# Sums of the opening's modulations formed as columns by TensorE, late operands pinned in the mixers, and later modulations in the merge

## The chip, the cores and the metric

The kernel runs on one core of a Trainium2 chip. The metric is the device time of one execution in microseconds (us), as the median of several runs; smaller is better. One further execution is taken with the hardware profiler, and its trace is what the views below read. The engines are TensorE (PE, the matrix engine; PEld is its weight load), VectorE (DVE), ScalarE (ACT), GpSimd (POOL) and SyncE (SP), whose queue issues most of the DMAs.

## The reference

One layer over 1024 latent tokens and 256 context tokens of width 1024: a half-step gated FFN, token mixers (a short gated convolution and grouped-query attention) merged by gates and an output projection, and a second half-step FFN. Each sub-layer is normalised and modulated: nine vectors of 1024 (shift, scale and gate, three times) come from SiLU(c) for the latents and from SiLU(c_ctx) for the context, by one product with `w_mod`.

```python
mod_lat = (jax.nn.silu(c) @ w_mod[layer] + b_mod[layer])[:, None, :]
mod_ctx = (jax.nn.silu(c_ctx) @ w_mod[layer] + b_mod[layer])[None, None, :]
ml = jnp.split(mod_lat, N_MOD, axis=-1)
mc = jnp.split(mod_ctx, N_MOD, axis=-1)
x = x + 0.5 * ml[2] * swiglu(modulate(rms_norm(x, norm1_g[layer]), ml[0], ml[1]),
                              ffn1_w_in[layer], ffn1_w_out[layer])
cx = cx + 0.5 * mc[2] * swiglu(modulate(rms_norm(cx, norm1_g[layer]), mc[0], mc[1]),
                                ffn1_w_in[layer], ffn1_w_out[layer])
hx = modulate(rms_norm(x, norm2_g[layer]), ml[3], ml[4])
hc = modulate(rms_norm(cx, norm2_g[layer]), mc[3], mc[4])
...
x = x + ml[5] * merge_branches(y_conv_l, o_l, gt_l, w_branch_conv[layer],
                               w_branch_attn[layer], w_out[layer])
x = x + 0.5 * ml[8] * swiglu(modulate(rms_norm(x, norm3_g[layer]), ml[6], ml[7]),
                              ffn2_w_in[layer], ffn2_w_out[layer])
return rms_norm(x, final_g)
```

With `modulate(h, shift, scale) = h * (1 + scale) + shift` and `swiglu(h, w_in, w_out) = (silu(a) * b) @ w_out`, a and b being the halves of `h @ w_in`. The context's merge and second FFN are not needed, as the layer is the last.

## The kernel before, in words

**Products.** Activations lie with the width over the 128 partitions, tokens along the row, in two chunks of 512 tokens, C0 and C1. A float32 operand is split into a high part rounded to the matmul's format (made by ACT, names ending in h, or the first of a pair) and a low part, the rest (made by DVE); a product is three matmuls, high by high, high by low and low by high. The large products (FFN1, the mixers' `w_in`, FFN2) are formed by the Winograd scheme of class `Winograd`: of the 2x2 blocks of weights and activations seven products are made, numbered 1 to 7, from sums and differences of blocks. Weights come as `raw` by DMA, `s` are sums of their blocks (POOL), `wl` the split weights; `r` are the split operands of the activations, `nt`, `t` and `h` the sums and blocks they are split from. `start` runs products 1 and 2 of the first `n_ahead` column pairs; `second` goes on with products 6, 7, 4 and the rest. While `start` runs, a generator (`norm`) makes the normalised operands of the later products, one step at each `run(norm, 1)`; its last steps make the operands of products 7, 4 and 3.

**Modulations.** They are made in three ways. In the opening, `column_mod` makes one half (512 columns) of modulations 1 and 0 for both streams by matmuls with `silu_c` (two columns, one per stream) as the loaded operand and `w_mod` (`rawm`) as the moving one; the result, two rows of 512, is copied by ACT (`mrow`) and transposed into columns, and `column_adds` adds the bias. `second_mod` makes the other half for the latents: DVE adds `rawm` times a scalar into `macc`, eight times, `acch` and `accl` are its split, two matmuls with a column of ones sum it over the partitions, and the row goes into columns as above. `later_mod` does likewise for all others, as a generator: eight steps that load a `rawm` and add it, four empty ones, the split, six empty ones, the sum, whose row goes into columns by small DMAs (`mcol`). Generators are pulled by `run(steps, n)`: `all_later_mods` in the loop of FFN1 over j, `STEPS[j]` steps a time and three in each pass of a side loop for the context, `late_steps` in the mixers' loop over i and in FFN2.

**Row products.** `row_products` multiplies the second matrix of an FFN: for each of the products 2, 1, 4, 6, 5, 7 and 3 over all its rows (`hid` from DRAM, split into `rh` and `rl`, weights `wl` and `wh`), and then adds the four results to their outputs (`add`, for instance x<-ps,gate_l,x). The context's own product is put among these as po<-hidc,wo, added into `cacc`.

**What sets the order.** The code issues instructions in order of its loops, and a scheduler moves them within each engine's stream. `pinned=True`, or `strict[0] = True` around a piece of code, keeps an instruction in the program's order. Buffers: `ttile` takes from one pool of 11 (macc, acch, accl, rawm, s, u, v and others share it); PSUM has five banks for ps, two for pt and one for po. All instructions go through one helper, so the line of nearly every row is 88, and rows are told apart by names.

Of the kernel before, what the change touches and what calls it, by code (L numbers as in the profile page):

```python
# [40 lines left out]
SIDE_FROM = 12  # L41
STEPS = (0, 4, 4, 4, 5, 5, 5, 5, 5, 5, 5, 2, 12)
WAIT = 4
# [6 lines left out]
def tile_dit_layer(  # L50
# [211 lines left out]
    def later_mod(m, halves=(0, 1), streams=None):  # L262
# [3 lines left out]
        for half in halves:  # L266
# [12 lines left out]
            for _ in range(WAIT):  # L279
                yield  # L280
            parts = []
            for acc in accs:
                ah, al = ttile("acch", dt=F32R), ttile("accl", dt=F32R)
                split(acc, ah, al)
                parts.append((ah, al))
            for _ in range(6):
                yield
            for (ah, al), v in zip(parts, streams):
                mod, pm = (modl, modc)[v], ps_t()
# [8 lines left out]
                dve.tensor_add(out=mod[:, c0 : c0 + 4], in0=mcol[:], in1=bcol[:, c0 : c0 + 4])  # L298
            yield

    def fetch_mod(m, half):
# [17 lines left out]
    def column_mod(m, half, raws, bank):  # L319

        sc = silu_c[:].rearrange("p (v k) -> p k v", k=KD)
        pr = bank()
        for k in range(KD):
            matmul(pr[:2], sc[:, k], raws[k // 2][:, k % 2], start=(k == 0), stop=(k == KD - 1))
            if k % 2 and k < KD - 1:
                yield
        row = ttile("mrow")
        act.copy(out=row[:2], in_=pr[:2])
        yield
        pm = ps_t(8)  # L330
        for j in range(4):
            transpose(pm[:, 2 * j : 2 * j + 2], row[:2, j * P : (j + 1) * P])
        column_adds(m, half, pm, (0, 1))
        yield

    def second_mod(m, half, raws):

        acc = ttile("macc")
        for k in range(KD):
# [15 lines left out]
        pm = ps_t(4)  # L355
        for j in range(4):
            transpose(pm[:, j : j + 1], row[:1, j * P : (j + 1) * P])
        column_adds(m, half, pm, (0,))
        yield
# [106 lines left out]
    class Winograd:  # L466
# [194 lines left out]
        def start(self, norm):  # L661

            for i in range(self.n_ahead):
                t = wpool.tile([P, 2, 512], F32, tag="wh", name=uniq("uc"), bufs=W_BUFS)
                u, c = t[:, 0], t[:, 1]
                act.copy(out=u, in_=self.product(1))
                run(norm, 2 if i == 0 else 1)
                dve.tensor_add(out=c, in0=u, in1=self.product(2))
                if i < RESIDENT:
                    self.started.append((u, c))  # L670
                else:
                    self.put_aside(t)
            run(norm, 9 - self.n_ahead)
            self.prefetch(4)
            self.late = norm
# [79 lines left out]
        def third(self, u, v):  # L755
# [39 lines left out]
    def row_products(w, rows, add, after=lambda i, k: None, halves=False):  # L795
# [112 lines left out]
        }  # L908
        chain = None
        for i in (2, 1, 4, 6, 5, 7) + (() if halves else (3,)):  # L910
# [3 lines left out]
            for g, (k, m) in enumerate(groups):  # L914
# [4 lines left out]
                strict[0] = True  # L919
                sums(i, g)  # L920
                strict[0] = False
                after(i, k)
            for o, ch in to[i]:
                for d in range(4):
                    add(o + d, ch, ps[d])
            after(i, rows.n)
        if halves:
            kept = []
            ps = [ps_s(256) for _ in range(4)]
            for k, m in groups:  # L930
                for lr in operands(3, k, m):
                    step(3, ps, len(kept), *lr, n=256)
                    kept.append(lr)
                after(8, k)
            for d in range(4):
# [110 lines left out]
    run(mod00)  # L1046
    part_gain(gain1["c"], 0, "g1", "c", 0, 4)
    mod11 = second_mod(1, 1, raws11)
    for k in range(4):
        left_operand(0, k, mod11)  # L1050
    start = half1.start_together()
    half1.prefetch(5, lo_engines=(pool, pool))
# [88 lines left out]
    def all_later_mods():  # L1141
# [153 lines left out]
    def after1(i, k):  # L1295
# [16 lines left out]
        if k == NH // 2:  # L1312
# [4 lines left out]
            elif i == 3:  # L1317
                done(range(4), C1)
        if i == 3 and k in (0, 4):
            run(norms2, 1)  # L1320
# [23 lines left out]
    for i in range(KD):  # L1344
# [581 lines left out]
```

## Time and profile before

| | us |
|---|---|
| median of 3 runs (2686.28 to 2688.88) | 2687.64 |
| the profiled run's own time | 2688.7 |
| its span in the trace | 2686.9 |
| PE busy | 2643.4 |
| DVE busy | 2007.1 |
| ACT busy | 1166.1 |
| POOL busy | 521.3 |
| mean granted clock of PE | 0.993 |

The stages follow one another on PE: opening (to about 60 us), FFN1 with the side loop (to 665), its row products (to about 935), the mixers, attention, the merge and the output projection (to about 2030), FFN2 and its row products (to the end). The granted clock is the share of full speed that PE was allowed in a stretch. In the timeline a row is a run of alike instructions with start and length; in brackets stands the idle time of the engine before it, and what ended it. A matmul's start-to-start distance can be less than its shown length, as they are pipelined.

### The profile page before, as it was taken

Reading aid. Unit: us, or ns where it says so; the run is one execution under the profiler, and the core shown is the slowest. Engines: PE = TensorE matmul, PEld = TensorE weight load, DVE = VectorE, ACT = ScalarE, POOL = GpSimd, SP = SyncE. Lnnn points to the kernel's source line nnn. Section 1 sums busy time; section 2 is a strip of 40 time slices with the busy share of each in tenths; the row PEclk is TensorE's granted clock in tenths of the full one; section 3 lists DMA queues with packets and bytes.
Section 4 is the critical chain, followed back from the end, with each engine's and each line's share of the span. In section 5 each row is a group of like instructions: output and inputs, shape, how many; then the busy total and the mean of one; then the engine's idle time right before and its main releaser. Section 6 shows DMA issues by size and latency. Waiting matters only on the chain.

```text
span 2686.9 us, 37399 instructions
## 1 busy us (share of the span) xinstructions
PE 2643.4 (98%) x13593; PEld 2236.0 (83%) x13593; DVE 2007.1 (75%) x3356; ACT 1166.1 (43%) x2317; POOL 521.3 (19%) x409
## 2 busy tenths in 40 slices
PE   8999999999999999999999999999999999999998
PEld 5788898888788877888999888877888888888888
DVE  5888888786887889877488666775458875667875
ACT  6633543333454632333244666674236333334543
POOL 1244012121110044232033111000001533230200
PEclk9999999999999999999999999999999999999998
DMA  7655653346973445433213211002524543228731
GB/s 267 236 180 166 223 184 124 109 130 240 293 169 102 149 137 165 134 114 116 97 48 103 95 62 49 24 25 78 167 85 146 184 145 99 83 90 305 165 83 63
DMA packets 369920, 364.84 MB, mean 136 GB/s; under 512 B 27830, under 2 KB 261448, under 8 KB 369736
## 3 DMA queue, kind: packets, MB, share of 16 engines
q1 hardware_dynamic: 360712, 345.17, 39.0%
q0 software_dynamic: 9024, 17.30, 4.0%
q8 instruction: 106, 1.74, 0.3%
q14 instruction: 78, 0.64, 0.1%
HBM read 296.30 MB, written 66.06 MB: 135 GB/s over the span
## 4 chain that ended last, share of the span: by engine, by line
PE 88%; DVE 6%; DMA 2%; ACT 2%; issue 1%; SPq 1%; POOL 0%; DVEq 0%; ACTq 0%; POOLq 0%
PE ps L88 73%; PE po L88 7%; PE pt L88 7%; DMA rawm<-in_w_mod_dram 1%; DVE macc L88 1%; DVE wl L88 1%; SPq L88 1%; DVE xb L88 0%; DVE r L88 0%; ACT r L88 0%; DMA raw<-in_ffn_w_in_dram 0%; DMA xtok<-in_ctx_dram 0%; DVE ol L88 0%; DVE x L88 0%; DVE pts L88 0%
## 5 line engine op out<-in xcount | busy, mean ns | idle before, releaser
L88 PE MATMUL ps<-r,wl 128*128 128x512 f32 x5232 | 1213.4, 392 | 11.6 <-ACT wl L88 6.8
L88 PEld LDWEIGHTS ps<-r,wl 128*128 128x128 f32 x5232 | 983.9, 189 | 220.0 <-ACT wl L88 9.0
L88 ACT CAST wl<-s 128x512 fp32r<-128x512 f32 x256 | 158.0, 620 | 338.3 <-PE ps L88 266.6
L88 POOL TENSOR_TENSOR s<-raw 128x512 f32<-128x512 f32 x64 | 92.4, 1444 | 993.8 <-PE ps L88 346.6
L88 ACT CAST wl<-raw 128x512 fp32r<-128x512 f32 x286 | 176.4, 619 | 250.0 <-PE ps L88 160.6
L88 DVE TENSOR_TENSOR wl<-raw,wl 128x512 fp32r<-128x512 f32 x284 | 202.6, 717 | 68.3 <-ACT wl L88 64.7
L88 DVE TENSOR_TENSOR wl<-s,wl 128x512 fp32r<-128x512 f32 x256 | 231.8, 906 | 12.3 <-ACT wl L88 10.7
L88 POOL TENSOR_TENSOR s<-raw,s 128x512 f32<-128x512 f32 x64 | 99.8, 1560 | 363.9 <-DVE wl L88 354.4
L88 DVE SCALAR_TENSOR_TENSOR macc<-rawm,silu_c,macc 128x512 f32<-128x512 f32 x168 | 137.9, 837 | 9.5 <-DMA rawm<-in_w_mod_dram 9.1
L88 PE MATMUL ps<-wh,r 128*128 128x256 f32 x768 | 141.6, 285 | 0.0
L88 DVE TENSOR_TENSOR pts<-pt,pts 128x512 fp32r<-128x512 f32 x160 | 108.8, 687 | 39.4 <-ACT pts L88 38.4
L88 DVE TENSOR_TENSOR u<-u,ps 128x512 f32<-128x512 f32 x168 | 114.2, 680 | 28.5 <-PE ps L88 28.4
L88 DVE TENSOR_REDUCE m<-ps 128x1 f32<-128x512 f32 (+1 forms) x192 | 110.9, 596 | 31.0 <-PE ps L88 30.3
L88 ACT CAST pts<-pt 128x512 fp32r<-128x512 f32 x160 | 93.2, 593 | 88.7 <-PE pt L88 86.8
L88 ACT CAST rh<-hid 128x512 fp32r<-128x512 f32 x132 | 81.6, 621 | 112.2 <-PE ps L88 96.2
L88 PE MATMUL ps<-rh,wl 128*128 128x512 f32 x360 | 122.0, 389 | 0.0
L88 PEld LDWEIGHTS ps<-wh,r 128*128 128x128 f32 x768 | 120.6, 192 | 0.0
L88 ACT CAST wh<-raw 128x512 fp32r<-128x512 f32 (+1 forms) x88 | 69.3, 795 | 103.0 <-PE ps L88 79.5
L88 PE MATMUL po<-pts,vh 128*128 128x512 f32 x256 | 110.5, 437 | 1.5 <-ACT pts L88 1.5
L88 DVE TENSOR_TENSOR rl<-hid,rh 128x512 fp32r<-128x512 f32 x132 | 90.1, 686 | 26.5 <-ACT rh L88 13.5
L88 PE MATMUL ps<-wl,r 128*128 128x256 f32 x384 | 108.8, 283 | 0.0
L88 PE MATMUL ps<-kl,qs 128*128 128x512 f32 x384 | 105.3, 397 | 0.0
(298 smaller groups left out, 5068.1 us busy)
## 6 DMA issues: line engine op xcount, KB each, us to landing
raw<-in_ffn_w_in_dram SPq DMA_DIRECT2D x125, 512.0 KB
raw<-in_ffn_w_out_dram SPq DMA_DIRECT2D x72, 512.0 KB
rawm<-in_w_mod_dram SPq DMA_DIRECT2D x128, 256.0 KB
raw<-in_w_in_dram SPq DMA_DIRECT2D x61, 512.0 KB
hid<-hd SPq DMA_DIRECT2D x40, 512.0 KB
ws<-in_ffn_w_out_dram POOLq DMA_DIRECT2D x30, 512.0 KB, 6.6
ucd<-uc SPq DMA_DIRECT2D x22, 512.0 KB
hd<-c SPq DMA_DIRECT2D x38, 256.0 KB
```

Of the source, the lines that this page charges most:

```text
L88: inst = getattr(self.engine, name)(*args, **kw)
```

## The change

The change has five parts.

1. In the opening, `column_mod` swaps the operands: blocks of `rawm` are loaded and the two columns of `silu_c` move, so the sum arrives as columns; the row's copy and its transposes are gone. `second_mod` sums `macc` the same way, against a column of ones, through the new `summed_mod`; its split, row and transposes are gone. `part_gain` for the context comes after the first left operand.
2. `later_mod` splits and sums one stream after the other, three empty steps behind each split.
3. `STEPS` is lower; m=5 moves from `all_later_mods` to `late_steps`, which is pulled less in the mixers (from i=3, two and two) and also in the merge, five steps behind each of 14 pieces.
4. `start` of the mixers takes no step of `norm` at i = 5, 6 and 8, and none at its end; `late_operands` runs the rest, pinned, inside the first `second`.
5. `row_products` adds a product's results behind the first sums of the next product, pinned (`add_results`), and the steps `norms2` come at k = 2 and 6.

```diff
-STEPS = (0, 4, 4, 4, 5, 5, 5, 5, 5, 5, 5, 2, 12)
+STEPS = (0, 3, 3, 4, 4, 4, 4, 4, 4, 4, 4, 4, 7)
...
-            parts = []
-            for acc in accs:
+            for acc, v in zip(accs, streams):
                 ah, al = ttile("acch", dt=F32R), ttile("accl", dt=F32R)
                 split(acc, ah, al)
-                parts.append((ah, al))
-            for _ in range(6):
-                yield
-            for (ah, al), v in zip(parts, streams):
+                for _ in range(3):
+                    yield
...
+    def summed_mod(m, half, accs, streams, bank, pinned):
+        nv = len(streams)
+        pm = bank(4 * nv)
+        for i, acc in enumerate(accs):
+            for j in range(4):
+                matmul(
+                    pm[:, nv * j + i : nv * j + i + 1], acc[:, j * P : (j + 1) * P], ones[:], start=True, stop=True,
+                    pinned=pinned,
+                )
+        column_adds(m, half, pm, streams)
...
-        pr = bank()
+        pm = bank(8)
         for k in range(KD):
-            matmul(pr[:2], sc[:, k], raws[k // 2][:, k % 2], start=(k == 0), stop=(k == KD - 1))
+            for j in range(4):
+                matmul(
+                    pm[:, 2 * j : 2 * j + 2], raws[k // 2][:, k % 2, j * P : (j + 1) * P], sc[:, k],
+                    start=k == 0 and j == 0, stop=k == KD - 1, on=j > 0,
+                )
             if k % 2 and k < KD - 1:
                 yield
-        row = ttile("mrow")
-        act.copy(out=row[:2], in_=pr[:2])
+        column_adds(m, half, pm, (0, 1))
         yield
-        pm = ps_t(8)
-        for j in range(4):
-            transpose(pm[:, 2 * j : 2 * j + 2], row[:2, j * P : (j + 1) * P])
-        column_adds(m, half, pm, (0, 1))
...
-        ah, al = ttile("acch", dt=F32R), ttile("accl", dt=F32R)
-        split(acc, ah, al)
         yield
-        pr = ps_s()
-        matmul(pr[:1], ones_r[:], ah, start=True, stop=False)
-        matmul(pr[:1], ones_r[:], al, start=False, stop=True)
-        row = ttile("mrow")
-        act.copy(out=row[:1], in_=pr[:1])
+        summed_mod(m, half, [acc], (0,), ps_s, False)
         yield
...
-                run(norm, 2 if i == 0 else 1)
+                run(norm, 2 if i == 0 else 0 if self.plain and i in (5, 6, 8) else 1)
...
-            run(norm, 9 - self.n_ahead)
...
-            run(self.late, 4)
+            self.late_operands(1)
             dve.tensor_add(out=v, in0=u, in1=self.product(7))
...
-            run(self.late)
+            self.late_operands()
             return v, b
+
+        def late_operands(self, n=None):
+            strict[0] = True
+            run(self.late, n)
+            strict[0] = False
...
+        chain, results = None, []
+
+        def add_results():
+            while results:
+                i, ps = results.pop()
+                for o, ch in to[i]:
+                    for d in range(4):
+                        add(o + d, ch, ps[d])
+                after(i, rows.n)
...
                 sums(i, g)
+                add_results()
...
-            for o, ch in to[i]:
-                for d in range(4):
-                    add(o + d, ch, ps[d])
-            after(i, rows.n)
+            results.append((i, ps))
+        if not halves:
+            add_results()
...
-        for m in range(2, 6):
+        for m in range(2, 5):
             yield from later_mod(m)
...
-    steps, late_steps = all_later_mods(), (step for m in (6, 7, 8) for step in later_mod(m))
+    steps, late_steps = all_later_mods(), (step for m in (5, 6, 7, 8) for step in later_mod(m))
...
-        if i > 1:
-            run(late_steps, 5)
+        if i > 2:
+            run(late_steps, 2)
         for ch, bg, gc in mixed():
-            if i > 1:
-                run(late_steps, 4)
+            if i > 2:
+                run(late_steps, 2)
...
                 run(merge(j, ch))
+                run(late_steps, 5)
```

The first place where the order shows it is PE in the opening. The names are out<-in: `xtok` are tokens being transposed, `rs_y` the norm of the rows, `r`,`wl` the first product. Before:

```order
L88 MATMUL ps_158<-ident,xtok_111 128x128
L88 MATMUL pt_175<-rawm_113,silu_c 2x512 x2
L88 MATMUL pt_179<-ident,rs_y_139 128x128 x4
L88 MATMUL pt_175<-rawm_115,silu_c 2x512 x2
L88 MATMUL pt_175<-rawm_117,silu_c 2x512 x2
L88 MATMUL pt_175<-rawm_119,silu_c 2x512 x2
L88 MATMUL po_205<-rawm_121,silu_c 2x512 x2
L88 MATMUL pt_217<-ident,mrow_203 128x2 x4
L88 MATMUL po_205<-rawm_123,silu_c 2x512 x2
L88 MATMUL po_205<-rawm_125,silu_c 2x512 x2
L88 MATMUL po_205<-rawm_127,silu_c 2x512 x2
L88 MATMUL ps_259<-ident,xtok_105 128x128
```

And now:

```order
L88 MATMUL ps_158<-ident,xtok_111 128x128
L88 MATMUL pt_175<-silu_c,rawm_113 128x2 x8
L88 MATMUL pt_185<-ident,rs_y_139 128x128 x4
L88 MATMUL pt_175<-silu_c,rawm_115 128x2 x8
L88 MATMUL pt_175<-silu_c,rawm_117 128x2 x8
L88 MATMUL pt_175<-silu_c,rawm_119 128x2 x8
L88 MATMUL po_229<-silu_c,rawm_121 128x2 x8
L88 MATMUL po_229<-silu_c,rawm_123 128x2 x8
L88 MATMUL po_229<-silu_c,rawm_125 128x2 x8
L88 MATMUL po_229<-silu_c,rawm_127 128x2 x8
L88 MATMUL ps_300<-ident,xtok_105 128x128
```

Each piece of `rawm` stood for two matmuls of 512 moving columns, and now stands for eight of two; the transposes of `mrow` are gone, and the norm's transposes keep their place.

The second place is ACT at the start of the mixers, where `start` ends: the last product 2 that it copies is in `uc`, and the split weights `wl` behind it belong to the first `second`. Before:

```order
L88 CAST r_1526_8821<-t_1511_8756 128x512
L88 CAST r_1534_8863<-t_1473_8587 128x512
L88 CAST r_1535_8866<-t_1485_8642 128x512
L88 CAST r_1536_8869<-t_1498_8699 128x512
L88 COPY uc_8955<-ps_8959 128x512
L88 CAST r_1537_8872<-t_1511_8756 128x512
L88 CAST r_1545_8914<-h_1472_8586 128x512
L88 CAST r_1546_8917<-h_1484_8641 128x512
L88 CAST r_1547_8920<-h_1497_8698 128x512
L88 CAST r_1548_8923<-h_1510_8755 128x512
L88 CAST wl_8936<-s_1552_8931 128x512
L88 CAST wl_8956<-s_1553_8932 128x512
```

And now:

```order
L88 CAST r_1497_8826<-t_1433_8523 128x512
L88 CAST r_1498_8829<-t_1445_8578 128x512
L88 CAST r_1499_8832<-t_1458_8635 128x512
L88 CAST r_1500_8835<-t_1471_8692 128x512
L88 COPY uc_8867<-ps_8871 128x512
L88 CAST wl_8848<-s_1504_8843 128x512
L88 CAST wl_8868<-s_1505_8844 128x512
L88 CAST wl_8885<-raw_8840 128x512
L88 CAST wl_8904<-s_1503_8842 128x512
L88 CAST r_1526_8932<-t_1433_8523 128x512
L88 CAST r_1527_8935<-t_1445_8578 128x512
L88 CAST r_1528_8938<-t_1458_8635 128x512
```

Twelve splits of `r` stood between `nt` and the first `wl<-s`, and now four do; the other eight come behind the weights, four of `t` behind four `wl`, and those of `h` after two more `wl`.

The third place is PE at the end of FFN1's first part: `ps<-r` is its last product, po<-hidc the context's product, pt<-acch and pt<-accl the sum of a later modulation, ps<-rh,wl the first row product. Before:

```order
L88 MATMUL ps_6514<-r_209_1011,wl_6450 128x512 x3
L88 MATMUL pt_6531<-acch_6288,ones_r 1x512
L88 MATMUL pt_6531<-accl_6289,ones_r 1x512
L88 MATMUL po_6632<-hidc_6222,wo_6542 128x256 x3
L88 MATMUL po_6632<-hidc_6222,wo_6548 128x256 x3
L88 MATMUL po_6632<-hidc_6222,wo_6542 128x256 x3
L88 MATMUL po_6632<-hidc_6222,wo_6548 128x256 x3
L88 MATMUL ps_6582<-rh_6591,wl_6588 128x512
L88 MATMUL ps_6583<-rh_6591,wl_6588 128x512
```

And now:

```order
L88 MATMUL ps_6423<-r_197_1027,wl_6359 128x512 x3
L88 MATMUL po_6568<-hidc_6116,wo_6452 128x256 x3
...
L88 MATMUL po_6568<-hidc_6116,wo_6458 128x256 x3
L88 MATMUL po_6582<-hidc_6116,wo_6452 128x256 x3
...
L88 MATMUL po_6610<-hidc_6116,wo_6461 128x256 x3
L88 MATMUL pt_6464<-acch_6448,ones_r 1x512
L88 MATMUL pt_6464<-accl_6449,ones_r 1x512
L88 MATMUL pt_6479<-acch_6475,ones_r 1x512
L88 MATMUL pt_6479<-accl_6476,ones_r 1x512
L88 MATMUL ps_6518<-rh_6527,wl_6524 128x512
L88 MATMUL ps_6519<-rh_6527,wl_6524 128x512
```

The four groups of four rows po<-hidc, of which three stood among the row products, now all stand ahead of them, and two sums of modulations instead of one do.

More of the change, by code (lines that the diff above doesn't have):

```diff
@@ L345, in second_mod @@
             yield
-        ah, al = ttile("acch", dt=F32R), ttile("accl", dt=F32R)
-        split(acc, ah, al)
         yield
-        pr = ps_s()
-        matmul(pr[:1], ones_r[:], ah, start=True, stop=False)
-        matmul(pr[:1], ones_r[:], al, start=False, stop=True)
-        row = ttile("mrow")
-        act.copy(out=row[:1], in_=pr[:1])
+        summed_mod(m, half, [acc], (0,), ps_s, False)
         yield
[L355 to L358, printed above, removed]
         yield
@@ L908, in row_products @@
         }
-        chain = None
+        chain, results = None, []
[6 more added lines that the diff above has]
+                after(i, rows.n)
         for i in (2, 1, 4, 6, 5, 7) + (() if halves else (3,)):
@@ L933, in row_products @@
                     kept.append(lr)
+                add_results()
                 after(8, k)
@@ L1046, in tile_dit_layer @@
     run(mod00)
-    part_gain(gain1["c"], 0, "g1", "c", 0, 4)
     mod11 = second_mod(1, 1, raws11)
@@ L1050, in tile_dit_layer @@
         left_operand(0, k, mod11)
+        if k == 0:
+            part_gain(gain1["c"], 0, "g1", "c", 0, 4)
     start = half1.start_together()
@@ L1318, in after1 @@
                 done(range(4), C1)
-        if i == 3 and k in (0, 4):
+        if i == 3 and k in (2, 6):
             run(norms2, 1)
```

## Prediction

> **What bounds the kernel now.** First the page: the busy shares and the chain that ended last.
>
> ```profile
> PE 2643.4 (98%) x13593; PEld 2236.0 (83%) x13593; DVE 2007.1 (75%) x3356; ACT 1166.1 (43%) x2317; POOL 521.3 (19%) x409
> PE 88%; DVE 6%; DMA 2%; ACT 2%; issue 1%; SPq 1%; POOL 0%; DVEq 0%; ACTq 0%; POOLq 0%
> ```
>
> TensorE (PE) is busy for 2643.4 of 2686.9 us, so only 43.5 us of idle time can go. Any other gain must come from PE's work or from its clock. The change adds and removes little work, so idle time and clock decide. For the clock I asked for narrow windows around the idle stretches, PE alone (columns: us, PE busy, granted clock, DMA share, GB/s).
>
> ```profile
> 28.00:40.00 12.00, 9.97 (x40) 0.86 1.07 394
> 700.00:712.00 12.00, 8.94 (x38) 1.00 0.82 241
> 943.00:953.00 10.00, 9.44 (x29) 0.67 0.49 156
> 1058.00:1068.00 10.00, 8.93 (x27) 0.66 0.43 133
> 2643.50:2645.90 2.40, 2.40 (x25) 1.00 0.00 0
> 2646.00:2648.00 2.00, 2.00 (x12) 0.50 0.00 0
> ```
>
> The clock drops to half behind each larger stall, though not behind the 3.06 us in two pieces of the second row. 10 x 0.33 = 3.3 us is lost after 943 and 10 x 0.34 = 3.4 after 1058; 12 x 0.14 = 1.7 after 28. The last two rows are the odd ones: PE is never idle there, and still the clock halves. The timeline says what ran:
>
> ```profile
> 2643.49 4.61 PE L88 MATMUL pt<-ones,sq 128*128 128x1 f32 x32
> ```
>
> 32 matmuls with a 128x128 operand loaded and one column moved through it. At full clock 25 of them fill 2.40 us in the window row. Each then costs about 0.11 us. In the next 2 us there are 12, products among them; 22 at 0.11 and 10 at 0.21 make 4.5, the row's 4.61. So a run of one-column matmuls made the clock fall about 2.4 us after its start, as idleness does. This carries the first term, since the change puts 128 instructions of nearly that shape into the opening.
>
> **Term 1, the first modulations (`column_mod`).** PE's timeline of the opening:
>
> ```profile
> 11.19 1.88 PE L88 MATMUL pt<-rawm,silu_c 128*2 128x512 f32 x4 [0.30 <-DMA rawm<-in_w_mod_dram]
> 13.78 5.31 PE L88 MATMUL pt<-rawm,silu_c 128*2 128x512 f32 x12
> 18.92 1.88 PE L88 MATMUL po<-rawm,silu_c 128*2 128x512 f32 x4
> 20.73 0.41 PE L88 MATMUL pt<-ident,mrow 2*128 2x2 f32 x4
> 21.07 5.31 PE L88 MATMUL po<-rawm,silu_c 128*2 128x512 f32 x12
> 26.31 1.09 PE L88 MATMUL ps<-ident,xtok 128*128 128x128 f32 x8
> 27.34 0.41 PE L88 MATMUL pt<-ident,mrow 2*128 2x2 f32 x4
> 29.45 0.50 PE L88 MATMUL ps<-r,wl 128*128 128x512 f32 x1 [1.71 <-ACT r L88]
> 30.53 7.14 PE L88 MATMUL ps<-r,wl 128*128 128x512 f32 x23 [0.58 <-DVE r L88]
> ```
>
> Before, 32 instructions take 1.88 + 5.31 + 1.88 + 5.31 = 14.4 us. A matmul of the order stands as two rows of the trace here, so the 64 new ones are 128 instructions: 128 x 0.11 = 14.1 us at full clock, no gain, while the 0.8 us of mrow transposes and a row's copy go. With the clock halved 2.4 us in, 22 run at 0.11 and 106 at 0.213: 2.4 + 22.6 = 25.0, or 10.6 more than 14.4. A first window that begins later gives some of it back; I take +9. Behind it, the 1.7 us wait for r shrinks under the xtok transposes, now twice as long, and the 24 products keep about as much half clock as the 1.7 us that they lose today. At the point where those products are done (37.67) I put the new kernel at +8. If the clock does not fall, the modulations end at 26.0 and r is there some 1.7 us later: about -2 to -3 at that point.
>
> The Trainium skill, "TensorE: Matmul & The Clock Gate", Part 1, speaks of an activity window of about 3.4 us, with an idle window leading to half rate; column matmuls issued back to back leave no idle PE, and by that wording the change would cost nothing here. The row at 2643.49 disagrees. Its Part 4 says that transpose-mode matmuls don't count as busy in the same way, so work that the gate overlooks is not foreign to the page. By the one term 1 is about -2.5, by the other +8.
>
> **Term 2, the second halves (`second_mod`).** The split of the sum and the row go, twice. The waits' view (engine, what for: us in total, times, longest) and the timeline:
>
> ```profile
> PE ps L88 <- ACT acch L88: 1.2, 2, 0.6
> PE ps L88 <- DVE accl L88: 0.7, 2, 0.3
> 43.50 0.39 PE L88 MATMUL ps<-accl,ones_r 128*1 128x512 f32 x1 [0.34 <-DVE accl L88]
> 47.46 0.40 PE L88 MATMUL pt<-ident,mrow 1*128 1x1 f32 x4
> ```
>
> 1.2 + 0.7 = 1.9 us of waits go. On PE two matmuls of about 0.4 and 0.4 us of transposes go per half, 2 x 1.0 to 1.2, and 2 x 8 x 0.11 = 1.8 come. I take -1.7 in all, between 0 (the column matmuls on half clock) and -2.5.
>
> **Term 3, the end of FFN1 (`STEPS`, `later_mod`).** The loop of FFN1 now pulls fewer steps than its modulations have: six steps are left over and run behind the loop, the two splits of m=4's second half among them. The order puts this on PE: four groups po<-hidc, the four matmuls of the two sums, and only then the first row product, ps<-rh,wl. Before, one group and one sum stood ahead of it:
>
> ```profile
> 664.64 0.40 PE L88 MATMUL pt<-acch,ones_r 128*1 128x512 f32 x1
> 665.11 1.60 PE L88 MATMUL po<-hidc,wo 128*128 128x256 f32 x12
> 665.31 0.58 ACT L88 COPY mrow<-pt 1x512 f32<-1x512 f32 x1 [2.26 <-PE pt L88]
> 666.55 1.13 PE L88 MATMUL ps<-rh,wl 128*128 128x512 f32 x4
> 669.36 1.59 PE L88 MATMUL po<-hidc,wo 128*128 128x256 f32 x12
> 703.11 0.50 PE L88 MATMUL pt<-rh,wl 128*128 128x512 f32 x1 [1.39 <-ACT wl L88]
> ```
>
> Then row products began 1.9 us after 664.64. Now VectorE (DVE) has 19 instructions to do, from the last adds of the loop to the second accl, before the last sum can be multiplied: adds of cacc, splits, four macc. Their starts lie 0.61 us apart when DVE is full:
>
> ```profile
> 706.18 0.68 DVE L88 TENSOR_TENSOR wl<-raw,wl 128x512 fp32r<-128x512 f32 x1
> 706.79 0.68 DVE L88 TENSOR_TENSOR wh<-raw,wh 128x512 fp32r<-128x512 f32 x1
> ```
>
> That is 19 x 0.61 = 11.6 us. Some 2.4 us of its waits come on top (for the first po group, for acch, and for the row copy of 0.58 that stands ahead of the second acch on ScalarE, ACT), then the matmul, the second row copy and rh, 0.4 + 0.6 + 0.6: row products begin about 15.6 us after that point. Of the 13.7 us more, 3 x 1.6 = 4.8 are po groups that only move forward, and 0.5 is the second sum: 8.4 us are idle. Within such a stretch PE is idle for more than half of a few microseconds, as it was at 943; one or two windows at half clock cost 1.7 to 3.4. The weights' DMA gains lead meanwhile, so the 1.39 at 703 goes. 8.4 + 2.6 - 1.4 is about +10. Bounds: +3, if DVE and PE are less full there than I count and the clock holds; +13, if the last two rawm loads, issued on SP's queue behind 13 hid and eight x loads, land late. Queued behind the waiting matmuls on PE is everything else; nobody can fill in.
>
> **Term 4, the start of the side loop.** The context's normalisation ends one pass of the loop later, so that the splits ahead of these waits spread out:
>
> ```profile
> 277.32 0.39 PE L88 MATMUL ps<-h1ch,wl 128*128 128x256 f32 x1 [1.13 <-ACT wl L88]
> 287.43 0.51 PE L88 MATMUL ps<-h1ch,wl 128*128 128x256 f32 x2 [1.80 <-DVE wl L88]
> ```
>
> Half of these 2.9 us: -1.5 (0 to -3).
>
> **Term 5, results of row products added later (`add_results`).**
>
> ```profile
> 701.81 2.72 DVE L88 SCALAR_TENSOR_TENSOR x<-ps,gate_l,x 128x512 f32<-128x512 f32 x4
> 706.92 0.73 PE L88 MATMUL pt<-rh,wl 128*128 128x512 f32 x2 [1.67 <-DVE wl L88]
> ```
>
> The four adds of 2.72 us stood ahead of the rl and wl that PE needed next; now they come behind them. -1.7 (0 to -3). The other changes of group had no such gap.
>
> **Term 6, the start of the mixers (`late_operands`).**
>
> ```profile
> 940.82 2.18 ACT L88 CAST r<-h 128x512 fp32r<-128x512 f32 x4
> 943.57 8.73 PE L88 MATMUL ps<-r,wl 128*128 128x512 f32 x25 [5.05 <-ACT wl L88]
> ```
>
> ACT made twelve r, at 2.18 / 4 = 0.55 each, before the first weights' split, wl<-s. In the order four r now stand ahead of the wl and eight follow behind: wl is ready 8 x 0.55 = 4.4 us earlier. What is late next is DVE's part of the same r and of the wl; I leave 2.2 of the 5.05 idle, in two pieces, like the 1.39 and 1.67 at 703 and 706.92, behind which the window row 700 to 712 shows a full clock; so the 3.3 us of half clock go too: -2.9 - 3.3 = -6.2. Bounds: -2.9 if the clock still falls, -8.4 if nothing waits.
>
> **Term 7, the stall in the mixers.**
>
> ```profile
> 1053.04 1.47 POOL L88 TENSOR_TENSOR s<-raw 128x512 f32<-128x512 f32 x1 [10.38 <-DVE accl L88]
> 1057.68 0.73 PE L88 MATMUL ps<-r,wl 128*128 128x512 f32 x2 [1.51 <-ACT wl L88]
> 1059.48 2.93 PE L88 MATMUL ps<-r,wl 128*128 128x512 f32 x6 [1.07 <-DVE wl L88]
> ```
>
> GpSimd (POOL) waited 10.38 us for a modulation's split, PE then 1.51 + 1.07, and the clock row prices the rest at 3.4. The step that made this split is no longer run in that pass (i=2), and two splits are left in the mixers where four were: -6.0 (0, if the same wait comes in another pass). The modulations put into the merge (70 steps, 35 loads of rawm, in 14 places) lie under PE work there:
>
> ```profile
> 1850.00:2000.00 150.00, 150.00 (x669) 124.29 (x668) 73.60 (x102) 39.50 (x52) 0.00 (x0) 1.00 0.45 141
> ```
>
> DVE is half free (73.6 of 150) and DMA too (0.45): 35 macc of some 0.7 us are 25 us in it. I cost them at nothing; without that cover, each split that PE waited for would cost as one in the opening, 0.9, and there are four.
>
> **Sum.** +8 - 1.7 + 10 - 1.5 - 1.7 - 6.2 - 6.0 = +0.9 us on the profiled run's 2688.7 (span 2686.9 and 1.8 around it): 2689.6. The median of the runs lies 1.1 below the profiled one, so the forecast for the median is 2687.64 + 0.9 = **2688.5**, with 2683 to 2694 as its own range. Two losses of about the size of the gains cancel them.
>
> **Rivals.**
> - *The clock holds in the columns* (chance 0.20): the gate counts a column matmul as work. Term 1 is -2.5 instead of +8, the time 2688.5 - 10.5 = 2678.0. For it: in the opening other work lies near, and its columns are two wide, not one. Against: the half-clock row behind 2643.49. The skill's wording of the gate is for it.
> - *The end of FFN1 hides its sums* (0.15): DVE comes to the macc earlier, because its loop has fewer modulation steps now. Term 3 is +3: 2681.5. Against: the adds of cacc wait for PE one by one, whatever DVE's load.
> - *The mixers' stall stays* (0.17, the slower side): the split that is begun in the mixers and read only in the merge keeps two buffers of the pool from which s, macc, acch and accl come. If POOL then finds none free for more than about 6 us, as in the 10.38 us wait above, term 7 is 0: 2694.5, slower than before.
> - *The late operands don't bring the start forward* (0.06): DVE's r is as late as ACT's wl was, the idle time stays near 4 us and the clock falls. Term 6 is -1: 2693.7.
>
> **Chances.** The forecast keeps 0.42. A measurement of this kernel can tell about 0.2%, 5.4 us, from no change: 2682.3 to 2693.0. The forecast gives 0.06 faster, 0.28 same, 0.08 slower; the clock that holds 0.17 and 0.03 same; the hidden sums 0.09 and 0.06 same; the stall that stays 0.04 same and 0.13 slower; the last 0.03 and 0.03. Together 0.32 faster, 0.44 same, 0.24 slower. The range, 2677 to 2697, takes in the two ends of term 1 and the stall that stays.
>
> **What would show it.** Term 1: the rawm,silu_c columns between 11 and 37 us, 0.21 apart from the third microsecond on, a granted clock well under 1 in that stretch and the first product near 38 to 39; near 28 means the first rival. Term 2: no acch among PE's waits in the opening. Term 3: PE idle 8 us in pieces between po<-hidc and ps<-rh,wl, released by cacc, acch and accl, and a granted clock under 1 behind. Term 5: no wait on wl behind x<-ps,gate_l. Term 6: the gap before the first ps<-r,wl of wl<-s near 2 us and clock 1.00 behind it. Term 7: no POOL wait on accl of 10 us. The prediction is wrong if the opening gains, if the end of FFN1 shows no new idle time, or if a stall of several microseconds turns up in merge or attention.

## The result, and the profile after

| | us |
|---|---|
| before, median of 5 runs (2681.91 to 2688.88) | 2686.28 |
| changed, median of 5 runs (2704.98 to 2710.98) | 2707.89 |
| ratio, 95% interval | 1.0081, 1.0067 to 1.0095 |
| the changed kernel's profiled run, its span | 2707.89, 2705.8 |

The changed kernel is slower by 0.8%, some 21 us; 2688.5 with a range up to 2697 was forecast. All times are medians, which one execution of 6605 us among the ten of a later run (the first under "Parts combined") does not move. The page of the changed kernel, busy shares and chain:

```profile
PE 2659.5 (98%) x13685; PEld 2261.3 (84%) x13685; DVE 2000.6 (74%) x3354; ACT 1164.0 (43%) x2311; POOL 520.7 (19%) x409
PE 85%; DVE 7%; DMA 3%; ACT 2%; issue 2%; SPq 1%; POOL 0%; DVEq 0%; ACTq 0%; POOLq 0%
```

PE's idle time went from 43.5 to 2705.8 - 2659.5 = 46.3 us, while its busy time rose by 16.1: most of the loss looks like work. To see where it lies, take one product that both kernels have (the nth matmul of the same operands) and compare its start in the two traces. The difference ("shift") is worked out so from the two timelines, and "step" is what a stretch adds to it:

| from, to (time of before) | shift there | step | forecast |
|---|---|---|---|
| opening, to 100 | +8.7 | +8.7 | +6.3 |
| FFN1 and side loop, to 664 | +8.8 | +0.1 | -1.5 |
| end of FFN1 and its row products, to 930 | +17.1 | +8.3 | +8.3 |
| start of the mixers, to 970 | +11.5 | -5.6 | -6.2 |
| next pass, to 1010 | +13.6 | +2.1 | 0 |
| stall at 1057 and the rest of the mixers, to 1450 | +6.1 | -7.5 | -6.0 |
| start of attention, to 1840 | +11.2 | +5.1 | 0 |
| merge, to 2030 | +20.9 | +9.7 | 0 |
| end of FFN2 | +19.4 | -1.5 | 0 |

The forecast had the losses of the opening and of FFN1's end and the gains of the mixers nearly right. It had 0 for attention and merge, where 14.8 us went.

**The opening.** PE's timeline of the changed kernel:

```profile
11.14 3.55 PE L88 MATMUL pt<-silu_c,rawm 128*128 128x2 f32 x16 [0.25 <-DMA rawm<-in_w_mod_dram]
14.55 1.09 PE L88 MATMUL pt<-ident,rs_y 128*128 128x128 f32 x4
15.44 10.24 PE L88 MATMUL pt<-silu_c,rawm 128*128 128x2 f32 x48
25.54 13.79 PE L88 MATMUL po<-silu_c,rawm 128*128 128x2 f32 x64
39.19 1.95 PE L88 MATMUL ps<-ident,xtok 128*128 128x128 f32 x8
40.82 7.16 PE L88 MATMUL ps<-r,wl 128*128 128x512 f32 x24
```

The 128 columns take 3.55 + 10.24 + 13.79 = 27.6 us, 0.21 to 0.22 each from the first on, and eight transposes take 1.95 that took 1.09. The first product comes at 40.82 instead of 29.45. There is no idle time to see: all of it counts as PE's busy time. The windows of the granted clock say 1.00 here, yet the same transposes take 1.8 times as long. The trace explains it: its record of the clock has its first entry, 1.00, only at 43.45 us (at 10.84 in the kernel before), and a window ahead of the first entry shows that entry's value.

**FFN1's end.** The same view:

```profile
673.48 1.59 PE L88 MATMUL po<-hidc,wo 128*128 128x256 f32 x12
675.85 1.70 PE L88 MATMUL po<-hidc,wo 128*128 128x256 f32 x12 [0.78 <-DVE cacc L88]
...
683.43 0.40 PE L88 MATMUL pt<-acch,ones_r 128*1 128x512 f32 x1 [0.95 <-ACT acch L88]
685.24 0.58 PE L88 MATMUL pt<-accl,ones_r 128*1 128x512 f32 x1 [1.42 <-DVE accl L88]
687.01 0.58 PE L88 MATMUL pt<-acch,ones_r 128*1 128x512 f32 x1 [1.18 <-ACT acch L88]
687.74 0.59 PE L88 MATMUL pt<-accl,ones_r 128*1 128x512 f32 x1
689.51 2.08 PE L88 MATMUL ps<-rh,wl 128*128 128x512 f32 x4 [1.18 <-ACT rh L88]
```

The waits come as forecast, piece by piece: cacc three times, acch, accl, acch, rh. From 673.48, where the first po begins, to 689.51 are 16.0 us; 15.6 were forecast. The clock's record stands at half from 685 to 695; how much of this is loss, for which 1.7 to 3.4 us were forecast, was not taken apart.

**Start of the mixers**, where the gap of 5.05 stood, and the pass behind it:

```profile
956.52 1.25 PE L88 MATMUL ps<-r,wl 128*128 128x512 f32 x4 [0.90 <-ACT wl L88]
958.78 1.42 PE L88 MATMUL ps<-r,wl 128*128 128x512 f32 x5 [1.01 <-DVE wl L88]
1001.69 1.66 PE L88 MATMUL ps<-r,wl 128*128 128x512 f32 x6 [1.69 <-DVE wl L88]
```

0.90 + 1.01 are left of 5.05 (2.2 were forecast), but a wait of 1.69 is new at 1001.69.

**Attention and merge.** The timeline of attention's start, three engines' rows out of many:

```profile
1464.51 3.17 SPq L88 DMA_DIRECT2D g<-gcd  x3
...
1467.78 0.38 SPq L88 DMA_DIRECT2D zd<-g  x1
...
1471.26 0.62 ACT L88 CAST qs<-q 128x512 fp32r<-128x512 f32 x1 [7.94 <-DMA zd<-g]
...
1474.78 0.62 PE L88 MATMUL ps<-kc,qs 128*128 128x256 f32 x3 [2.97 <-ACT pc L88]
```

SP's queue is stuck 3.17 us at loads of g, the store zd<-g behind them comes late, ACT waits 7.94 us for the buffer that it frees, and PE waits 2.97 for ACT's pc. In the kernel before, qs waited 2.46 us there and PE not at all:

```profile
1459.69 0.62 ACT L88 CAST qs<-q 128x512 fp32r<-128x512 f32 x1 [2.46 <-DMA zd<-g]
```

The merge:

```profile
1939.90 9.55 SPq L88 DMA_DIRECT2D raw<-in_w_out_dram  x2
...
1949.51 0.57 SPq L88 DMA_DIRECT2D ga<-gad  x1
...
1953.59 0.69 DVE L88 TENSOR_TENSOR ga<-ga,ps 128x512 f32<-128x512 f32 x1 [4.54 <-DMA ga<-gad]
...
1954.33 0.50 PE L88 MATMUL ps<-mh,wh 128*128 128x512 f32 x1 [2.83 <-DVE ga L88]
```

Two weight loads of the output projection hold SP's queue for 9.55 us, ga is issued behind them, DVE waits 4.54 us for it and PE 2.83 for the bank that DVE frees. Before, two weight loads held the queue for even longer, but the last ga stood ahead of them, and DVE, which needed it at 1933.38, waited there for PE:

```profile
1907.62 0.32 SPq L88 DMA_DIRECT2D ga<-gad  x1
...
1914.20 11.26 SPq L88 DMA_DIRECT2D raw<-in_w_out_dram  x2
...
1933.38 0.69 DVE L88 TENSOR_TENSOR ga<-ga,ps 128x512 f32<-128x512 f32 x1 [2.65 <-PE ps L88]
```

### The profile page after: what moved, and what is told of

The parts are those of the page before. It is cut to its first block, busy times and chain, and to the rows that moved or that the text cites. A ratio compares the mean times of both kernels' runs of the same rounds, so it can differ in the third digit from the quotient of the medians.

```text
span 2705.8 us, 37518 instructions
## 1 busy us (share of the span) xinstructions
PE 2659.5 (98%) x13685; PEld 2261.3 (84%) x13685; DVE 2000.6 (74%) x3354; ACT 1164.0 (43%) x2311; POOL 520.7 (19%) x409
## 4 chain that ended last, share of the span: by engine, by line
PE 85%; DVE 7%; DMA 3%; ACT 2%; issue 2%; SPq 1%; POOL 0%; DVEq 0%; ACTq 0%; POOLq 0%
PE ps L88 69%; PE po L88 8%; PE pt L88 8%; DVE wl L88 1%; DMA rawm<-in_w_mod_dram 1%; SPq L88 1%; DVE r L88 1%; DMA raw<-in_ffn_w_in_dram 1%; DVE macc L88 0%; DMA x<-xd 0%; DVE nt L88 0%; DVE t L88 0%; DVE uc L88 0%; DVE u L88 0%; DVE pts L88 0%
## 5 line engine op out<-in xcount | busy, mean ns | idle before, releaser
L88 DVE TENSOR_TENSOR wl<-s,wl 128x512 fp32r<-128x512 f32 x256 | 220.4, 862 | 18.2 <-ACT wl L88 16.4
```

The costliest lines, as they stand in the source:

```text
L88: inst = getattr(self.engine, name)(*args, **kw)
```

## The experiments

The theory is that four separate places lose: columns at half clock, six steps left over at FFN1's end, a pair of buffers held through attention, and ga's place on SP's queue in the merge. Each run is the changed kernel with one part altered, but where it says otherwise. "Less" and "more" are against 2707.9. The kernel before was timed again beside each group of runs (medians of 2685.0 to 2687.2), the changed kernel was not; differences of 2 or 3 us are therefore not clear of noise, and there only the traces speak.

### The rows of the opening again

```diff
-        pm = bank(8)
...
+        pr = bank()
+        for k in range(KD):
+            matmul(pr[:2], sc[:, k], raws[k // 2][:, k % 2], start=(k == 0), stop=(k == KD - 1))
...
+        row = ttile("mrow")
+        act.copy(out=row[:2], in_=pr[:2])
```

> Only column_mod is put back to its form of before (two rows, copy, transposes); all other parts of the change stay. Theory, the 128 column matmuls leave the clock at half: they go back to 14.4 us and the first ps<-r,wl to about 29.5 instead of 40.82, the time falls by 9 to 11 us against the changed kernel's 2707.9, to about 2698. Rival, the opening is late for another reason (DMA, the weights' split): the first product stays behind 35 and the time within 3 us of 2707.9.

2696.3 (ratio to before 1.0035, 1.0023 to 1.0046), 11.6 less, a little more than forecast. The first product comes at 31.97. So the columns themselves cost this; DMA does not.

### How many columns move

```diff
-                    pm[:, 2 * j : 2 * j + 2], raws[k // 2][:, k % 2, j * P : (j + 1) * P], sc[:, k],
+                    pm[:, WIDE * j : WIDE * (j + 1)], raws[k // 2][:, k % 2, j * P : (j + 1) * P], sc_wide[:, k],
```

sc_wide holds silu_c's two columns over and over.

> column_mod keeps its columns, but 64 columns move through each loaded block instead of two (silu_c's two, 32 times over; only the first two are read). Theory, the clock is granted by how long columns move, not by how many matmuls are issued: 64 columns keep it up, the columns stand 0.11 to 0.14 apart once it is up, the first ps<-r,wl comes before 33 us and the time falls by 6 to 10 us to about 2699. Rival, loading the blocks is what keeps the clock down: they stay 0.21 or more apart, the first product at 40 or later, the time 2707 or more.

64 columns: 2709.2 (1.0089, 1.0074 to 1.0104). The theory's numbers fail, and the columns stand as far apart as with two. PE's timeline:

```profile
12.10 3.65 PE L88 MATMUL pt<-scw,rawm 128*128 128x64 f32 x16 [0.30 <-DVE rs_a L88]
...
16.39 10.34 PE L88 MATMUL pt<-scw,rawm 128*128 128x64 f32 x48
26.52 13.86 PE L88 MATMUL po<-scw,rawm 128*128 128x64 f32 x64
```

> As the run with 64 columns, with 128. If the clock is granted by how long columns move, there is a width at which it comes up, and 128 is the widest that fits a bank: the columns stand 0.11 to 0.14 apart within a few microseconds, and the first ps<-r,wl comes before 35. If loading the blocks keeps it down, they stay 0.21 to 0.28 apart and the first product comes at 41 or later.

128 columns: one run, 2695.5, about 12 less. The same blocks are loaded as often, and yet:

```profile
11.08 3.75 PE L88 MATMUL pt<-scw,rawm 128*128 128x128 f32 x16 [0.25 <-DMA rawm<-in_w_mod_dram]
...
15.18 5.52 PE L88 MATMUL pt<-scw,rawm 128*128 128x128 f32 x48
20.54 7.31 PE L88 MATMUL po<-scw,rawm 128*128 128x128 f32 x64
27.68 1.04 PE L88 MATMUL ps<-ident,xtok 128*128 128x128 f32 x8
29.33 0.50 PE L88 MATMUL ps<-r,wl 128*128 128x512 f32 x1 [0.61 <-ACT r L88]
```

The first 16 take 0.23 each, the next 48 0.115: the clock has come up. Sixty-four times the arithmetic takes 16.6 us instead of 27.6. The time is that of one run, but the clock's record agrees in every trace: its first entry lies between 42.94 and 46.09 us in the nine kernels that move 2 or 64 columns, at 14.85 with 128, and between 10.84 and 16.34 in the four that move rows of 512. So the clock follows how many columns move through the array in a stretch, not how many matmuls are issued nor how much is loaded; the width from which it comes up lies between 64 and 128 here.

### No step left over behind FFN1

```diff
-STEPS = (0, 3, 3, 4, 4, 4, 4, 4, 4, 4, 4, 4, 7)
+STEPS = (0, 3, 3, 4, 4, 4, 4, 4, 4, 4, 4, 4, 9)
```

> Only the last number of STEPS is raised from 7 to 9, so that no step is left over behind FFN1's loop and no sum stands between its last product and the row products. Theory, the six left-over steps make the stall: no PE wait on cacc, acch or accl at 675 to 690 and no half clock behind it, the row products begin some 10 us earlier, the time falls by 8 to 11 us to about 2698. Rival, the waits on cacc come from the context's product itself: the pieces of 0.8 us stay and the gain is under 4 us.

2706.0 (1.0072, 1.0056 to 1.0087), only 1.9 less. The stall does go: between 640 and 697 this kernel wins 12 us. But two waits that the changed kernel doesn't have come back 20 us later, with half clock behind them:

```profile
716.46 0.50 PE L88 MATMUL pt<-rh,wl 128*128 128x512 f32 x1 [1.23 <-ACT wl L88]
...
720.44 0.73 PE L88 MATMUL pt<-rh,wl 128*128 128x512 f32 x2 [1.87 <-DVE wl L88]
```

By 737 the win is 5.5 us. The rest is lost again in stretches that the edit doesn't touch (its opening began 2 us later, behind a late xtok). So in this trace the six steps cost 5.5 us, not 10, as the waits on wl return without them.

### The adds of row products at once again

The loop of the last experiment, with row_products (and the places of `norms2`) as before:

```diff
-            results.append((i, ps))
+            for o, ch in to[i]:
+                for d in range(4):
+                    add(o + d, ch, ps[d])
+            after(i, rows.n)
```

> STEPS ends in 9 as in the run with longer steps (2706.0), and add_results is undone as well, so that results of row products are added at once as before. Theory of the prediction, the four adds hold up wl and cost PE 1.7 us: the time is 1.5 to 3 us above 2706.0. Rival, that wait is set by the weights' DMA, since with longer steps a gap of 1.87 stood at 720.44 in spite of add_results: within 1 us of 2706.0, with a gap of about the same size there.

2703.6 (1.0068, 1.0051 to 1.0085). Its trace has the same pair:

```profile
712.38 0.50 PE L88 MATMUL pt<-rh,wl 128*128 128x512 f32 x1 [1.23 <-ACT wl L88]
...
716.35 0.73 PE L88 MATMUL pt<-rh,wl 128*128 128x512 f32 x2 [1.87 <-DVE wl L88]
```

1.23 and 1.87, to the hundredth what stands there with add_results. The reason is in DVE's rows: with add_results (the run with longer steps) three of the four adds still stand ahead of the wl that PE waits for:

```profile
715.33 2.06 DVE L88 SCALAR_TENSOR_TENSOR x<-ps,gate_l,x 128x512 f32<-128x512 f32 x3
...
719.70 0.68 DVE L88 TENSOR_TENSOR wl<-raw,wl 128x512 fp32r<-128x512 f32 x1
```

and without it they stand as far ahead:

```profile
711.24 2.06 DVE L88 SCALAR_TENSOR_TENSOR x<-ps,gate_l,x 128x512 f32<-128x512 f32 x3
...
715.61 0.69 DVE L88 TENSOR_TENSOR wl<-raw,wl 128x512 fp32r<-128x512 f32 x1
```

So the edit moves nothing at this wait, and the two runs can't tell whether the adds cause it. The time is 2.4 below 2706.0, as neither side had it, and the intervals overlap. In the traces the same two waits have half clock behind them (3.4 us) with add_results and none without, and the win by 737 is 7.1 us here against 5.5.

### The sum ready before attention

```diff
                 gate(gad, i, ch, g1)
+    run(late_steps, 2)
```

> Two more late steps are run behind the mixers' loop, so that the split begun there is summed before attention and gives back its two buffers; the merge goes on two steps further. Theory, the two buffers held through attention delay g<-gcd, zd<-g and qs: the gaps of 2.97 at 1474.78 and 1.40 at 1525.73 go, and the time falls by 4 to 5 us to about 2703. Rival, the start of attention is late for another reason (its order moved): the gaps stay and the time is within 1 us of 2707.9 but for the merge.

2698.8 (1.0044, 1.0029 to 1.0060), 9.1 less. Both gaps of attention's start are gone, and the shift falls by 5.0 us there: the split left open through attention, with its two buffers, was the cause. Two things more happened. The late steps stand two further on in the merge, other loads fall behind raw<-in_w_out, and the merge's gaps go too (7.7 less). But the first macc are now put among attention's last operations, and one of them waits on DVE for its rawm, with the softmax's pts behind it:

```profile
1809.49 0.75 DVE L88 SCALAR_TENSOR_TENSOR macc<-rawm,silu_c,macc 128x512 f32<-128x512 f32 x1 [1.90 <-DMA rawm<-in_w_mod_dram]
1810.16 1.28 DVE L88 TENSOR_TENSOR pts<-pt,pts 128x512 fp32r<-128x512 f32 x2
...
1810.90 0.71 PE L88 MATMUL pt<-ident,pl 128*128 128x128 f32 x4 [2.10 <-DVE pts L88]
```

The end of attention gives back 5.1. So in this trace the two ends of attention cancel, and what the time gains is the merge's, which the theory had not counted.

### The late steps in the output projection

```diff
                 run(merge(j, ch))
-                run(late_steps, 5)
+                run(late_steps, 2 if (j, ch) == (0, C1) else 0)
...
+            if ch == C0:
+                run(late_steps, 9)
```

> The merge runs two late steps (the sum already split) and no more; the others are run in the first half of the output projection, nine behind each of eight products, and gain3 is made behind them. Theory, what costs is that rawm loads and sums share SP's queue and the pool with ga and z, so that ga lands late: the gaps of 0.61, 2.83 and 0.67 and the half clock at 1941 to 1962 go, and the time falls by 6 to 8 us to about 2701. Rival, it is the work of the modulations itself (four sums on PE, DVE's macc) that costs: the loss moves to the output projection and the time stays within 2 us of 2707.9.

2715.9 (1.0111, 1.0093 to 1.0130), 8 more. The loss of the merge goes: between 1904 and 2025 this kernel wins 8 us, although the sums still run in that stretch, in the projection now. Then FFN2's start, whose squares and norm were hidden in the projection's second half, is mixed with the last of these steps on DVE (the last macc begins at 2028.74), and PE waits for it:

```profile
2030.74 1.05 PE L88 MATMUL pt<-ones,sq_acc 128*128 128x1 f32 x8 [1.74 <-DVE sq_acc L88]
2034.11 1.09 PE L88 MATMUL pt<-ident,rs_y 128*128 128x128 f32 x4 [2.32 <-DVE rs_y L88]
2037.47 3.75 PE L88 MATMUL ps<-r,wl 128*128 128x512 f32 x7 [2.27 <-ACT r L88]
```

The clock's record stands at half from 2032 to 2049 behind these waits. The run is a loss for a reason that neither side had named; whether fewer steps at a time would do was not tried.

### ga on another queue

```diff
-        sp.dma_start(out=ga, in_=gad[j, :, o : o + 512])
-        sp.dma_start(out=z, in_=zd[j, :, o : o + 512])
+        pool.dma_start(out=ga, in_=gad[j, :, o : o + 512])
+        pool.dma_start(out=z, in_=zd[j, :, o : o + 512])
```

> Only the loads of ga and z in the merge go from SP's queue to POOL's. Theory, in the changed kernel ga stands on SP's queue behind two weight loads of the output projection that wait 8.9 and 9.6 us for a buffer, and PE waits for ga: the gaps at 1941 to 1962 (0.61, 2.83, 0.67) and the half clock go, the time falls by 4 to 7 us against 2707.9. Rival, ga is late because the pool of eleven buffers is full of rawm, or DVE is late: the gaps stay near 4 us in sum and the time is within 2 us of 2707.9.

2706.0 (1.0073, 1.0057 to 1.0089), 1.9 less, short of 4 to 7. The three gaps are gone all the same, and the shift falls by 5.9 us between 1915 and 1987; SP's queue was the cause. The profiled run lost 3.9 us on the way there, in stretches that the edit doesn't touch (its opening, a half clock behind 1002 and another behind 1477).

### The later modulations as before

STEPS, later_mod and the places of late_steps as in the kernel before; columns, late operands and add_results of the change.

> Part 3 of the change is undone whole (STEPS, later_mod, m=5 and the places of late_steps as before); columns, late operands and add_results stay. By the shifts between the two traces: opening +8, end of FFN1 back to before, start of the mixers about -4 to -6, the stall at 1057 back (+6), attention and merge as before: 2687 to 2692. If the late modulations were not the cause of the losses behind the mixers, the 5 us in attention and 8 in the merge stay: 2700 or more.

2690.0 (1.0015, 1.0006 to 1.0024), 17.9 less. So moving the modulations costs 18 of the 21 us in sum, its gain in the mixers already taken off. The stall at 1060 is back, but without half clock in this trace:

```profile
1060.59 0.73 PE L88 MATMUL ps<-r,wl 128*128 128x512 f32 x2 [2.03 <-ACT wl L88]
1062.39 3.93 PE L88 MATMUL ps<-r,wl 128*128 128x512 f32 x16 [1.07 <-DVE wl L88]
```

The 3.4 us of clock that the seventh term counted on were not a fixed price.

### The late operands undone

start's steps and second's `run(self.late, 4)` as before.

> Only late_operands and the steps left out in start are undone on the changed kernel. Theory, the operands moved behind the weights bring the mixers' start forward: the gap of 5 us before the first ps<-r,wl of the mixers' second product comes back, with half clock behind it, and the time is 3 to 7 us over 2707.9. Rival, the gain at the start of the mixers only moves on to 1001.69 and comes from the later modulations: within 2 us of 2707.9.

2710.6 (1.0094, 1.0080 to 1.0108), 2.7 more, between the two sides. The gap comes back at 5.07 with half clock behind it, 5.1 us by the shift, but the one at 1001.69 goes (2.0), as it isn't in before either. So the operands' move is worth about 3 us, not 6: a part of the wait only went on to the next pass.

### Parts combined

The rows of the opening, STEPS with the numbers of before, and two more steps ahead of attention:

> The changed kernel with column_mod in its form of before, STEPS with the numbers of before, and two more late steps behind the mixers' loop. If the parts add up: 10 to 11.6 (opening) and 8 to 9 (sum before attention) less, and 2 to 6 less from FFN1's end and the side loop: 2682 to 2687, about the time of before (2687.2). If the late modulations' new places cost beyond that: 2690 or more.

2686.9 (1.0001, 0.9991 to 1.0011): the parts add up, to the time of before and no better. To it, the late steps in the merge moved to a later place, and ga and z on POOL's queue:

```diff
-                run(late_steps, 5)
+                run(late_steps, 6 if j > 1 else 0)
```

> The combined kernel (2686.9) with two changes more: in the merge the late steps begin with the third column (six behind each of twelve pieces, none before), so that no macc waiting for rawm stands among attention's last operations on DVE, and ga and z are loaded by POOL's queue. Theory, each late modulation's loss is where it stands in a queue: the gaps of 1.10 and 1.84 at 1792 to 1795 go, no gap of ga comes back, and the time falls by 3 to 5 us, to 2682 to 2684, below before. Rival, the sums and macc cost the same wherever they stand: 2686 or more.

2678.1 (0.9973, 0.9963 to 0.9982), 7 below before, and more than the 3 to 5 us that were forecast. Attention's end and the merge, which has four sums and their macc in it:

```profile
1750.00:1850.00 100.00, 94.78 (x530) 76.29 (x529) 69.44 (x124) 58.77 (x126) 2.69 (x5) 1.00 0.13 40
1850.00:2000.00 150.00, 150.00 (x669) 123.36 (x668) 98.98 (x149) 43.37 (x59) 11.88 (x22) 1.00 0.63 200
```

In the merge PE is busy for 150.00 of 150 us with 25 us more of DVE's work than before (98.98 against 73.60). The same two stretches of the first combined kernel, and the merge of the changed kernel:

```profile
1750.00:1850.00 100.00, 91.49 (x508) 72.52 (x507) 71.36 (x126) 58.73 (x124) 0.00 (x0) 1.00 0.15 46
1850.00:2000.00 150.00, 150.00 (x666) 123.20 (x665) 93.09 (x138) 41.31 (x56) 0.00 (x0) 1.00 0.59 188
...
1850.00:2000.00 150.00, 145.68 (x641) 117.72 (x642) 92.21 (x131) 38.63 (x52) 0.00 (x0) 0.99 0.63 200
```

The room in the merge was there: from 1840 to 2030 the last kernel loses 2.0 us to the kernel before, and four sums are 1.8 of them. Against the first combined kernel it gains at attention's end (94.78 against 91.49); the merge was full there already, so what POOL's queue for ga adds to it is not shown. One kernel was not tried: rows in the opening with the later modulations as before. If the gains of those two runs add up (11.6 and 17.9), it takes 2678.4, so that moving modulations into the merge pays at all is not shown.

## Why the prediction was wrong

- **The step that failed** is in term 7: "I cost them at nothing", of the modulations put into the merge. Busy shares (DVE 73.6 of 150, DMA 0.45) said that there was room, and there was. But a transfer is late by what stands ahead of it in its queue and by the buffer that it waits for. The step that moved loads onto SP's queue was not followed to what stands behind them, ga. That is 9.7 us, of which five sums of two matmuls at 0.23 are 2.3, the gaps 4.1 and half clock behind them 1.7; the 1.6 left were not taken apart. The prediction had named a stall in merge or attention as a sign of being wrong, but no term held its price.
- **A rival was right, but at another place.** "The mixers' stall stays" had the mechanism, two buffers held by a split that is read only in the merge, but put it in the mixers on POOL. It struck on SP, ACT and PE at attention's start, 5.1 us, which the sum didn't have at all.
- **Term 1** held, and was 2.4 too small with term 2: the clock did not fall 2.4 us into the columns, it never came up, so that all 128 ran at 0.21. The rival in which the gate counts a column matmul as work fell: 2 or 64 columns left the clock down, and only 128 brought it up. The Trainium skill, "TensorE: Matmul & The Clock Gate", Part 1, has the clock depend on how busy PE has been recently; by PE's timeline it was never idle between 11 and 41, and ran at half speed.
- **Term 2**: no acch is left among the opening's waits, as forecast. It was not tried alone.
- **Term 3** was right as a stall (16.0 us against 15.6), and the trace's net with the row products is the forecast's +8.3. That the sum agreed is partly luck: taken away, the stall gives back 5.5 us in one trace and 7.1 in another, since waits of 1.2 + 1.9 us return at 716 to 722, of which term 5 claimed 1.7 for add_results.
- **Term 4** was wrong: the normalisation that ends one pass later made its own waits there (h1cl, 2.3 us in two pieces, and half clock).
- **Term 5** failed in the step "now they come behind them": where the wait returned, DVE ran three of the adds 4.37 us ahead of the wl with add_results and without. In the changed kernel the wait is gone, as forecast, but behind the stall of term 3. Whether the adds set the wait stays open.
- **Term 6** was right in its mechanism and size at its place (-5.6), but 2.1 of it came back at 1001.69; undone alone, it is about 3.
- **Term 7**'s gain came in the trace (-6.5 at 1057), with half of it hanging on where the clock fell.

## What to carry to other kernels

Work moved into a stage with free engines is priced by its queue and its buffers: list what is issued behind each moved DMA and which tiles stay alive across the next stage, then the free share. A stall that is taken away shows the one behind it, so a term is worth what is left after the next wait. Many matmuls with few moving columns were dear in this opening, as the clock stayed down for the transposes behind them as well.

## What the runs showed of the hardware

- 128 matmuls with 128x128 loaded ran at about 0.215 us each with 2 columns and with 64, and at 0.115 with 128 once the clock was up (27.6, 27.9 and 16.6 us in all): more columns, less time.
- The record of the granted clock read 1.00 in an opening where transposes took 1.95 us for 1.09. Its first entry stands at 43.45 us, where the clock came up; a clock that starts low has to be seen in the durations.
- The same 1.07 + 1.5 to 2.0 us of idle time at 1058 to 1062 left half clock for 6.8 us in one trace and none in another, with other stretches ahead of it. Two waits of 1.23 and 1.87 left 3.4 us of half clock behind 716 to 722 in one trace and none in the next. Idle time of this length has no fixed price here.
